# Hybrid trunk layer: first modulation blocks loaded ahead of the first weights, and S5 output products taking turns on the two row halves

## The chip, the cores and the metric

The kernel runs on one core of a Trainium2 chip. The metric is device time in microseconds (us), from the first to the last instruction of the core and the little that lies around it; the median of several runs counts, and lower is better. The engines named below are TensorE (PE, with its weight loads PEld), VectorE (DVE), ScalarE (ACT), GpSimd (POOL) and SyncE (SP, which issues nearly all transfers). Each engine works through its own instructions in a fixed order; a wait of one instruction holds everything behind it on that engine.

## What is computed

One pre-norm residual layer on `x` (1024 positions, 1024 channels, float32), with adaLN modulation. Of the reference, this matters here:

```python
mod = (cond @ ada_w[l] + ada_b[l])[:, None, :]
sh1, sc1, g1, sh2, sc2, g2 = jnp.split(mod, 6, axis=-1)
u = rmsnorm(h, norm_mix_w[l]) * (1.0 + sc1) + sh1
proj = u @ w_in[l]
...
# S5: a complex diagonal scan per group, then
y = (jnp.einsum('bsgp,ghp->bsgh', st_re, c_re.astype(f32))
     - jnp.einsum('bsgp,ghp->bsgh', st_im, c_im.astype(f32)))
y = y.reshape(bsz, s, S5_WIDTH) + d_skip.astype(f32) * uf
g = jax.nn.gelu(y)
...
h = h + g1 * (groups @ w_out[l])
v = rmsnorm(h, norm_mlp_w[l]) * (1.0 + sc2) + sh2
h = h + g2 * (jnp.square(jax.nn.relu(v @ mlp_w1[l])) @ mlp_w2[l])
```

`u` feeds one input projection; its columns go to a pooling, a gated convolution, an SSD and an S5 mixer, whose outputs are concatenated, projected and followed by an MLP.

## The kernel before

Every float32 product is made of three products of rounded halves: operands are split into a high part (`uh`, `wh_...`, a cast, mostly on ACT) and the remainder (`ul`, `wl_...`, a subtraction on DVE), and PE computes high x high, high x low and low x high. A Tile scheduler orders the instructions of each engine, from the code's order, priorities and its own estimate of times; `tc.issue_after(i)` says that what is inside is to be placed behind instruction `i`, `tc.high_priority()` that it goes ahead of what else is ready.

In order of time:

- 0 to about 100 us, the x projection. Rows 0 to 511 of `x` (tiles `x0` to `x3`, `h=0`) are normalised on DVE, then for each of eight channel blocks `k` two blocks of the modulation matrix (`ada1_k`, the scale, and `ada0_k`, the shift) are reduced on DVE (`ada_block`, L326), `modulation` makes `amul` (L337) and `ash` (L339), `modulated_T` transposes the four x tiles on PE into `tp_u` (L363), ACT makes `uh` (L365) and the unrounded `t32` (L368), DVE `ul` (L371), and PE runs the products `pjx` (L638 to L640) with the weights of `split_xw` (L590). Then the same for rows 512 to 1023 (`h=1`, tiles `x4` to `x7`). Their normalisation needs a square sum on ACT and a power on POOL (`rs_u`, L347 and L348). Within `h=1` each `k` also reduces two more modulation blocks (`ada2_k`, `ada4_k`). Beside all this DVE works off some hundred small operations (`s5_small`: `s5ar`, `elo`, `ehi`, ...) for the S5 tables.
- 100 to about 260 us, the other projections (`pjs`, `zp`, `pjpl`, `pjgc`, `pjgh`, `pjgb`) and between them the two halves `b=0` and `b=1` of the S5 channels (`s5_half`): input products into `s5sr` and `s5si`, a scan on DVE that yields `s5xr` and `s5xi`, output products into the banks `s5y{b}0` and `s5y{b}1`, a GELU (`s5sq`, `s5th`, `s5g` on ACT and DVE), transposes `s5gp`, and the GLU. A bank `s5y{b}{g2}` takes, for each of four `q`, two products with 64 contraction rows (X0: L503, X1: L504; rows 0 to 63 for `g2=0` and 64 to 127 for `g2=1`) and a 128-row product T (L505).
- 260 to about 400 us, the SSD chunks (`sdd`, `sds`, `sdt`, `sy`) among the output projection `o` (L959 to L961). Sums of squares for the group norms are narrow products `bss` (L851).
- 400 us to the end, the MLP.

Loads go through SP's queue in the order of issue: before the change `ws_x0` (the first weights), then `ada1_0`, `ada0_0`, `ws_x1` and so on.

Of the kernel before, what the change touches and what calls it, by code (L numbers as in the profile page):

```python
# [21 lines left out]
P = 128  # L22
# [29 lines left out]
def body(ctx: ExitStack, tc: tile.TileContext, x, c, pk, adaT, w_x, w_zd, w_pl, w_gl, w_in, w_out, w1, w2, fnw, out):  # L52
    nc = tc.nc
    V, A, PE, G, SY = nc.vector, nc.scalar, nc.tensor, nc.gpsimd, nc.sync
# [14 lines left out]
    def bank(name, tag="ms"):  # L69
        return pp.tile([P, 512], F32, tag=tag, name=name)  # L70
# [25 lines left out]
    xt = [gran(f"x{tb}", tag="x") for tb in range(NB)]  # L96
# [212 lines left out]
    for h in range(2):  # L309
        ps = bank(f"cb{h}", "pj")  # L310
# [8 lines left out]
    def ada_load(s, j, tag="m"):  # L319
        t = gran(f"ada{s}_{j}", tag=tag)  # L320
        lastload[0] = SY.dma_start(out=t, in_=adaT[s * 8 + j])
        return t

    def ada_block(s, j, t):
        col = mod[:, s * 8 + j:s * 8 + j + 1]
        V.scalar_tensor_tensor(out=t, in0=t, scalar=0.5, in1=cond, op0=MUL, op1=MUL, accum_out=col)  # L326

    amul = small("amul", 8)
    ash = small("ash", 8)
# [5 lines left out]
    def modulation(s_sh, s_sc, j, mulcol, shcol, wname):  # L335
        i, k = s_sc * 8 + j, s_sh * 8 + j
        V.scalar_tensor_tensor(out=mulcol[:, j:j + 1], in0=mod[:, i:i + 1], scalar=adab1[:, i:i + 1],  # L337
                               in1=pv(wname, j, j + 1), op0=ADD, op1=MUL)
        V.tensor_tensor(out=shcol[:, j:j + 1], in0=mod[:, k:k + 1], in1=pv("ada_b", k, k + 1), op=ADD)  # L339
# [19 lines left out]
    def modulated_T(n, k, h, mulcol, shcol, hi, lo, nm, act, t=None):  # L359

        ps = bank(f"tp_{nm}{k}{h}")
        for t4 in range(4):
            PE.transpose(ps[:, t4 * P:(t4 + 1) * P], n[h * 4 + t4][:, k * P:(k + 1) * P], ident)  # L363
        m, b = mulcol[:, k:k + 1], shcol[:, k:k + 1]
        A.activation(out=hi[:, H[h]], in_=ps, func=AF.Identity, scale=m, bias=b)  # L365
        t = t or half(f"t32_{nm}{k}{h}")
        if act:
            A.activation(out=t, in_=ps, func=AF.Identity, scale=m, bias=b)  # L368
        else:
            V.tensor_scalar(out=t, in0=ps, scalar1=m, scalar2=b, op0=MUL, op1=ADD)  # L370
        return V.tensor_tensor(out=lo[:, H[h]], in0=t, in1=f(hi[:, H[h]]), op=SUB)  # L371
# [91 lines left out]
    def s5_half(b, tables, Vb, GT):  # L463

        WT, CP, T, (ct, st) = tables
        ug = lambda g: Vb[:, g * P:(g + 1) * P]
        Zr, Zi, t1, t2 = (half(f"s5{n}{b}") for n in ("zr", "zi", "t1", "t2"))
        pr, pi = bank(f"s5sr{b}"), bank(f"s5si{b}")
        for q in range(4):
            for g2 in range(2):  # L470
                for w_, o in ((WT[0], pr), (WT[1], pi)):
                    PE.matmul(o[64 * g2:64 * g2 + 64, q * P:(q + 1) * P],
                              w_[:, q * P + 64 * g2:q * P + 64 * g2 + 64], ug(2 * q + g2), start=True, stop=True)
        tt(pr, ct, MUL, o=t1)
        tt(pi, st, MUL, o=t2)
        tt(t1, t2, ADD, o=Zr)
        tt(pi, ct, MUL, o=t1)
        tt(pr, st, MUL, o=t2)
        tt(t1, t2, SUB, o=Zi)
        for z in (Zr, Zi):  # L480
            for q in range(4):
                sl = slice(q * P, (q + 1) * P)
                V.tensor_tensor_scan(out=z[:, sl], data0=prm["mag8"][:, 4 * b + q:4 * b + q + 1].to_broadcast([P, P]),
                                     data1=z[:, sl], initial=0.0, op0=MUL, op1=ADD)

        q3 = lambda t: t.rearrange("p (q c) -> p q c", q=4)
        X = [half(f"s5xr{b}"), half(f"s5xi{b}")]
        for xx, a, c_, op in ((X[0], ct, st, SUB), (X[1], st, ct, ADD)):
            V.memset(q3(xx)[:, :, 0:1], 0.0)
            tt(Zr, a, MUL, o=t1)  # L490
            tt(Zi, c_, MUL, o=t2)
            last = V.tensor_tensor(out=q3(xx)[:, :, 1:128], in0=q3(t1)[:, :, 0:127], in1=q3(t2)[:, :, 0:127], op=op)
        Gs = gran(f"s5g{b}", tag="g5")
        c0 = math.sqrt(2.0 / math.pi)
        v8 = lambda t: t.rearrange("p (i e) -> p i e", i=8)

        for g2 in range(2):
            ps = bank(f"s5y{b}{g2}")
            s_ = slice(64 * g2, 64 * g2 + 64)
            for q in range(4):  # L500
                o = ps.rearrange("p (i g e) -> p i g e", i=8, g=4)[:, :, q, :]
                qs = slice(q * P, (q + 1) * P)
                PE.matmul(o, X[0][s_, qs], CP[0][s_, qs], start=True, stop=False)  # L503
                PE.matmul(o, X[1][s_, qs], CP[1][s_, qs], start=False, stop=False)  # L504
                PE.matmul(o, ug(2 * q + g2), T[g2][:, qs], start=False, stop=True)  # L505

            a_, b_ = half(f"s5sq{b}{g2}"), half(f"s5th{b}{g2}")
            A.activation(out=a_, in_=ps, func=AF.Square)
            V.tensor_scalar(out=a_, in0=a_, scalar1=0.044715 * c0, scalar2=c0, op0=MUL, op1=ADD)
            tt(a_, ps, MUL, o=b_)  # L510
            A.activation(out=b_, in_=b_, func=AF.Tanh)
            V.scalar_tensor_tensor(out=v8(Gs)[:, :, g2 * 64:(g2 + 1) * 64], in0=v8(b_), scalar=1.0, in1=v8(ps),
                                   op0=ADD, op1=MUL)
        gt3 = GT.rearrange("p (c i) -> p i c", i=8)
        for h in range(2):
            ps = bank(f"s5gp{b}{h}")
            for i4 in range(4):
                i = h * 4 + i4
                PE.transpose(ps[:, i4 * P:(i4 + 1) * P], Gs[:, i * P:(i + 1) * P], ident)
            A.copy(out=gt3[:, h * 4:(h + 1) * 4, :], in_=ps.rearrange("p (i c) -> p i c", i=4))  # L520
        return last
# [53 lines left out]
    def load_xw(k):  # L575
        t = wp.tile([P, 1024], F32, tag="ws", name=f"ws_x{k}", bufs=2)
        SY.dma_start(out=t[:, 0:768], in_=w_x[k])
        return t
# [18 lines left out]
    ada_tag = ("m", "g5")  # L597
    uh = [gran(f"uh{k}", F32R, "u") for k in range(NB)] if False else []
    ul = []
    ready(range(4))  # L600
    xb = []
    for h in range(2):
        if h == 0:
            ps = [bank(f"pjx{i}{h}", "pj" if i < 4 else "ms") for i in range(NX)]
        for k in range(NB):
            if h == 0:
                t = load_xw(k)
                ab = [ada_load(e, k, ada_tag[e]) for e in (1, 0)]
                if k == XAT:
                    with tc.issue_after(lastload[0].ins):  # L610
                        load_x(range(4, NB))
                split_xw(k, t)
                for e in (1, 0):
                    ada_block(e, k, ab[1 - e])
                modulation(0, 1, k, amul, ash, "nw")
                uh.append(gran(f"uh{k}", F32R, "u"))
                ul.append(gran(f"ul{k}", F32R, "u"))
            elif k == 0:
                with tc.issue_after(lastload[0].ins):
                    if XAT >= NB:  # L620
                        load_x(range(4, NB))
                    SY.dma_start(out=pk2, in_=pk[:, first:])
                    plw = small("plw", 256)
                    SY.dma_start(out=plw, in_=w_pl)
                ready(range(4, NB))
            modulated_T(xt, k, h, amul, ash, uh[k], ul[k], "u", True)
            if h == 1 and k == 0:
                for i in range(NX):
                    xb.append(gran(f"xb{i}", tag="x" if i < 4 else "m"))
                    A.copy(out=xb[i][:, H[0]], in_=ps[i])  # L630
                ps = [bank(f"pjx{i}{h}", "pj" if i < 4 else "ms") for i in range(NX)]
            if h == 1:
                for e in (2, 4):
                    ada_block(e, k, ada_load(e, k, "g5"))
            for i in range(NX):
                wh, wl, o = xw_of(k, i)
                c_ = slice(o, o + P)
                PE.matmul(ps[i], wh[:, c_], uh[k][:, H[h]], start=(k == 0), stop=False)  # L638
                PE.matmul(ps[i], wh[:, c_], ul[k][:, H[h]], start=False, stop=False)
                PE.matmul(ps[i], wl[:, c_], uh[k][:, H[h]], start=False, stop=(k == NB - 1))  # L640
# [27 lines left out]
    for b in range(2):  # L668
        ps = proj(8 + b, f"s5{b}")
# [13 lines left out]
    for q in range(8):  # L683
        ps = bank(f"zp{q}", "pj")
        o, ts_ = ps[:, 0:NZ], slice(q * P, (q + 1) * P)
# [78 lines left out]
    ps = bank("sfx")  # L764
# [15 lines left out]
    for q in range(8):  # L780
# [5 lines left out]
        for src, nm in ((ah, "Rh"), (al, "Rl")):  # L786
            o = half(f"{nm}{q}", F32R)
# [717 lines left out]
```

## Time and profile before

| what | value |
| --- | --- |
| runs | 1039.15, 1042.04, 1044.17 us; median 1042.04 us |
| profiled execution | 1042.58 us, of which 1040.7 us are the span from first to last instruction (1.9 us lie around it) |
| mean granted TensorE clock | 0.997 |
| PE busy | 1007.8 us (97% of the span) |
| DVE busy | 767.8 us (74%) |
| ACT, POOL busy | 497.9 us (48%), 48.4 us (5%) |

The span is nearly all PE. So the rows to look for are those where PE idles, and behind each of them the instruction that it waited for. In a timeline a row gives start, busy time, engine, line, operation, tiles without buffer numbers, shapes, the count of records put together, and in brackets the idle time before it and what ended that.

### The profile page before, as it was taken

How to read it: one execution, taken by the hardware profiler on the slowest of the kernel's cores; microseconds unless marked ns; L12 is line 12 of the kernel's file. 1: busy time of each engine (PE TensorE's matmuls, PEld its weight loads, DVE VectorE, ACT ScalarE, POOL GpSimd, SP SyncE). 2: the span in 40 equal slices, each digit the busy share in tenths (PEclk: the TensorE clock that was granted, in tenths of full speed). 3: DMA queues.
4: the chain of work that ended last, by engine and by line, in shares of the span. 5: the costliest groups of instructions: out<-in, count | busy, mean ns of one | idle time of the engine just before them, and what ended most of it. 6: DMA issues, size and time to landing. Idle time of an engine off the chain costs nothing.

```text
span 1040.7 us, 13216 instructions
## 1 busy us (share of the span) xinstructions
PE 1007.8 (97%) x4790; PEld 824.7 (79%) x4790; DVE 767.8 (74%) x1361; ACT 497.9 (48%) x825; POOL 48.4 (5%) x80
## 2 busy tenths in 40 slices
PE   4999999999999999999999999999999999999997
PEld 2777897776888888788888888887888888787886
DVE  8999959777788778986667667556644866567884
ACT  5644622315743426765556556564443443433642
POOL 2200000000020112000000000000000000000031
PEclk9999999999999999999999999999999999999999
DMA  9973311125321124145545554378975466787112
GB/s 362 335 259 126 101 45 41 61 64 172 130 114 41 41 75 168 31 152 182 182 163 194 189 186 147 134 300 307 386 280 186 144 200 209 254 305 257 43 52 110
DMA packets 62179, 175.07 MB, mean 168 GB/s; under 512 B 6529, under 2 KB 11137, under 8 KB 62114
## 3 DMA queue, kind: packets, MB, share of 16 engines
q1 hardware_dynamic: 61474, 173.07, 48.1%
q10 hardware_dynamic: 576, 1.05, 0.3%
q8 instruction: 37, 0.61, 0.2%
q14 instruction: 28, 0.23, 0.1%
q0 software_dynamic: 64, 0.11, 0.0%
HBM read 135.17 MB, written 39.04 MB: 167 GB/s over the span
## 4 chain that ended last, share of the span: by engine, by line
PE 77%; DVE 10%; DMA 8%; issue 2%; ACT 2%; POOL 0%; SPq 0%; POOLq 0%; DVEq 0%; ACTq 0%
PE q L1085 6%; PE q L1086 6%; PE q L1084 6%; PE px L1084 5%; PE px L1086 5%; PE px L1085 5%; DMA b12T<-in_w_dram 3%; DMA b21B<-in_w_dram 3%; PE o L959 3%; PE o L960 3%; PE o L961 3%; PE pz L1084 2%; PE pz L1086 2%; PE pz L1085 2%; DVE ada L326 2%; PE pjgh L547 2%
## 5 line engine op out<-in xcount | busy, mean ns | idle before, releaser
L1085 PE MATMUL q<-l_BT,h_AS 128*128 128x512 f32 x192 | 75.2, 392 | 1.2 <-DVE l_BT L1011 1.2
L1086 PE MATMUL q<-h_BT,l_AS 128*128 128x512 f32 x192 | 74.7, 389 | 0.0
L1010 ACT CAST h_AS<-aS 128x1024 fp32r<-128x1024 f32 x32 | 33.6, 1054 | 84.3 <-PE q L1085 69.9
L1084 PE MATMUL q<-h_BT,h_AS 128*128 128x512 f32 x192 | 64.0, 389 | 0.0
L1011 DVE TENSOR_TENSOR woS<-w,woS 128x512 fp32r<-128x512 f32 x60 | 41.2, 691 | 30.7 <-ACT woS L1010 30.7
L1010 ACT CAST woS<-w 128x512 fp32r<-128x512 f32 x60 | 37.2, 624 | 49.7 <-PE px L1086 25.6
L1011 DVE TENSOR_TENSOR l_A<-a,h_A 128x1024 fp32r<-128x1024 f32 x24 | 29.4, 1224 | 38.2 <-ACT h_A L1010 35.1
L1011 DVE TENSOR_TENSOR l_AS<-aS,h_AS 128x1024 fp32r<-128x1024 f32 x32 | 39.0, 1222 | 19.2 <-ACT h_AS L1010 18.9
L959 PE MATMUL o<-wh_wo,yh 128*128 128x512 f32 x128 | 52.5, 410 | 0.1
L960 PE MATMUL o<-wl_wo,yh 128*128 128x512 f32 x128 | 51.8, 405 | 0.0
L961 PE MATMUL o<-wh_wo,yl 128*128 128x512 f32 x128 | 50.8, 401 | 0.0
L1010 ACT CAST h_A<-a 128x1024 fp32r<-128x1024 f32 x24 | 25.2, 1052 | 53.0 <-PE q L1085 44.2
L1085 PE MATMUL q<-l_BB,h_A 128*128 128x512 f32 x128 | 50.0, 391 | 0.5 <-DVE l_BB L1011 0.5
L1086 PE MATMUL q<-h_BB,l_A 128*128 128x512 f32 x128 | 49.8, 389 | 0.0
L138 DVE TENSOR_TENSOR u<-u,pz 128x512 f32<-128x512 f32 x30 | 20.6, 687 | 39.1 <-ACT u L1156 29.0
L1084 PE MATMUL px<-vT,woS 128*128 128x512 f32 x120 | 46.8, 390 | 0.0
L1086 PE MATMUL px<-vT,woS 128*128 128x512 f32 x120 | 46.7, 389 | 0.0
L1085 PE MATMUL px<-vT,woS 128*128 128x512 f32 x120 | 46.7, 389 | 0.0
L966 DVE SCALAR_TENSOR_TENSOR h<-o,br,h 128x512 f32<-128x512 f32 x48 | 35.8, 748 | 11.5 <-PE o L961 11.2
L1085 PEld LDWEIGHTS q<-l_BT,h_AS 128*128 128x128 f32 x192 | 36.0, 188 | 10.2 <-DVE l_BT L1011 2.8
L1084 PE MATMUL q<-h_BB,h_A 128*128 128x512 f32 x128 | 42.6, 390 | 0.6 <-ACT h_BB L1010 0.6
L1010 ACT CAST wo<-w 128x512 fp32r<-128x512 f32 x45 | 27.8, 624 | 30.6 <-PE pz L1086 16.6
(513 smaller groups left out, 2934.0 us busy)
## 6 DMA issues: line engine op xcount, KB each, us to landing
ada<-in_ada_dram SPq DMA_DIRECT2D x32, 512.0 KB, 5.1
aS<-spS SPq DMA_DIRECT2D x32, 512.0 KB, 4.3
w<-in_w_dram SPq DMA_DIRECT2D x30, 512.0 KB, 3.5
spS<-s SPq DMA_DIRECT2D x48, 256.0 KB, 2.2
a<-sp SPq DMA_DIRECT2D x24, 512.0 KB, 5.7
b21B<-in_w_dram SPq DMA_DIRECT2D x16, 512.0 KB, 6.8
b22T<-in_w_dram SPq DMA_DIRECT2D x16, 512.0 KB, 3.6
sp<-u SPq DMA_DIRECT2D x30, 256.0 KB, 2.0
```

The lines of the kernel that those rows point to most:

```text
L138: (eng or V).tensor_tensor(out=o, in0=a, in1=b, op=op)
L326: V.scalar_tensor_tensor(out=t, in0=t, scalar=0.5, in1=cond, op0=MUL, op1=MUL, accum_out=col)
L547: PE.matmul(ps[h], w_[:, ks], u_[:, H[h]], start=(a and first), stop=(b and last))
L959: PE.matmul(ps, yh_, wo[b][0][:, H[h]], start=(b == 0), stop=False)
L960: PE.matmul(ps, yh_, wo[b][1][:, H[h]], start=False, stop=False)
L961: PE.matmul(ps, yl_, wo[b][0][:, H[h]], start=False, stop=(b == 1))
L966: V.scalar_tensor_tensor(out=hh, in0=ps, scalar=r[:, tb:tb + 1], in1=hh, op0=MUL, op1=ADD)
L1010: A.copy(out=hi, in_=t)
L1011: return V.tensor_tensor(out=lo, in0=t, in1=f(hi), op=SUB)
L1084: PE.matmul(ps, wh, ub, start=first, stop=False, skip_group_check=more)
L1085: PE.matmul(ps, wh, lb, start=False, stop=False, skip_group_check=more)
L1086: PE.matmul(ps, wl, ub, start=False, stop=last, skip_group_check=more)
```

## The change

Three edits. First, for `k=0` the two modulation blocks are loaded ahead of the first weights, and `modulation` of `h=0` runs at high priority. Second, for `h=1` the reductions of `ada2_k` and `ada4_k` are placed behind `ul_k` of the same block (the loads are issued as before). Third, both S5 output banks are allocated first; for `b=0` the X products of the two row halves take turns for each `q`, followed by both T products; for `b=1` the order stays (bank by bank), but all products are written ahead of the GELU code.

```diff
+        banks_ = [bank(f"s5y{b}{g2}") for g2 in range(2)]
+        outs = [[ps.rearrange("p (i g e) -> p i g e", i=8, g=4)[:, :, q, :] for q in range(4)] for ps in banks_]
+        if b == 0:
+            steps = [[(q, 0), (q, 1)] for q in range(4)]
+        else:
+            steps = [[(q, g2)] for g2 in range(2) for q in range(4)]
+        for step in steps:
+            for r in range(2):
+                for q, g2 in step:
+                    s_, qs = slice(64 * g2, 64 * g2 + 64), slice(q * P, (q + 1) * P)
+                    PE.matmul(outs[g2][q], X[r][s_, qs], CP[r][s_, qs], start=(r == 0), stop=False)
+            for q, g2 in step:
+                PE.matmul(outs[g2][q], ug(2 * q + g2), T[g2][:, q * P:(q + 1) * P], start=False, stop=True)
         for g2 in range(2):
-            ps = bank(f"s5y{b}{g2}")
-            s_ = slice(64 * g2, 64 * g2 + 64)
-            for q in range(4):
-                o = ps.rearrange("p (i g e) -> p i g e", i=8, g=4)[:, :, q, :]
-                qs = slice(q * P, (q + 1) * P)
-                PE.matmul(o, X[0][s_, qs], CP[0][s_, qs], start=True, stop=False)
-                PE.matmul(o, X[1][s_, qs], CP[1][s_, qs], start=False, stop=False)
-                PE.matmul(o, ug(2 * q + g2), T[g2][:, qs], start=False, stop=True)
+            ps = banks_[g2]
...
+                if k == 0:
+                    ab = [ada_load(e, k, ada_tag[e]) for e in (1, 0)]
                 t = load_xw(k)
-                ab = [ada_load(e, k, ada_tag[e]) for e in (1, 0)]
+                if k:
+                    ab = [ada_load(e, k, ada_tag[e]) for e in (1, 0)]
...
-                modulation(0, 1, k, amul, ash, "nw")
+                with tc.high_priority():
+                    modulation(0, 1, k, amul, ash, "nw")
...
-            modulated_T(xt, k, h, amul, ash, uh[k], ul[k], "u", True)
+            lo_ = modulated_T(xt, k, h, amul, ash, uh[k], ul[k], "u", True)
...
             if h == 1:
-                for e in (2, 4):
-                    ada_block(e, k, ada_load(e, k, "g5"))
+                ab = [ada_load(e, k, "g5") for e in (2, 4)]
+                with tc.issue_after(lo_.ins):
+                    for e in (2, 4):
+                        ada_block(e, k, ab[e // 2 - 1])
```

The scheduler reorders more than these lines; no engine's number of instructions or columns changes. Lines of the changed kernel are 7 higher from L513 on and 14 higher behind the x projection's loop (L503 to L505 become L508 and L510).

DVE at the start, before: the first weights' low parts, `x3`, the two blocks, then the second weights' low parts ahead of `ash`.

```order
L590 TENSOR_TENSOR wl_x0_380<-ws_x0_372,wh_x0_378 128x512
L138 TENSOR_TENSOR s5ar0_91<-s5ar0_91 128x8
L571 TENSOR_SCALAR x3_82<-x3_82,rs_u3_362 128x1024
L153 SCALAR_TENSOR_TENSOR s5ar0_91<-s5ar0_91 128x8
L590 TENSOR_TENSOR wl_y0_381<-ws_x0_372,wh_y0_379 128x256
L326 SCALAR_TENSOR_TENSOR ada1_0_374,mod_323<-ada1_0_374,cond_314 128x1024
...
L326 SCALAR_TENSOR_TENSOR ada0_0_376,mod_323<-ada0_0_376,cond_314 128x1024
L337 SCALAR_TENSOR_TENSOR amul_324<-mod_323,adab1_328,pkt_72 128x1
L153 SCALAR_TENSOR_TENSOR s5ar0_91<-s5ar0_91 128x8 x3
L590 TENSOR_TENSOR wl_x0_380<-ws_x1_419,wh_x0_378 128x512
L590 TENSOR_TENSOR wl_y0_381<-ws_x1_419,wh_y0_379 128x256
L339 TENSOR_TENSOR ash_325<-mod_323,pkt_72 128x1
```

And now: one low part of the first weights stands ahead of `ash`, the other and both of the second weights behind it.

```order
L326 SCALAR_TENSOR_TENSOR ada1_0_372,mod_323<-ada1_0_372,cond_314 128x1024
L145 TENSOR_SCALAR s5ar0_91<-s5ar0_91 128x8 x2
L578 TENSOR_SCALAR x3_82<-x3_82,rs_u3_362 128x1024
L337 SCALAR_TENSOR_TENSOR amul_324<-mod_323,adab1_328,pkt_72 128x1
L153 SCALAR_TENSOR_TENSOR s5ar0_91<-s5ar0_91 128x8
L326 SCALAR_TENSOR_TENSOR ada0_0_374,mod_323<-ada0_0_374,cond_314 128x1024
L138 TENSOR_TENSOR s5ar0_91<-s5ar0_91 128x8
L153 SCALAR_TENSOR_TENSOR s5ar0_91<-s5ar0_91 128x8
L597 TENSOR_TENSOR wl_x0_380<-ws_x0_376,wh_x0_378 128x512
L339 TENSOR_TENSOR ash_325<-mod_323,pkt_72 128x1
L597 TENSOR_TENSOR wl_y0_381<-ws_x0_376,wh_y0_379 128x256
```

PE at the S5 output products of `b=0`, now, from the first X1 on (before, all of bank `s5y00` stood ahead of the rest of `s5y01`, each `q` as X0, X1, T):

```order
L508 MATMUL s5y00_1620<-cpi0_1483,s5xi0_1610 128x8x16
L508 MATMUL s5y01_1621<-cpi0_1483,s5xi0_1610 128x8x16
L510 MATMUL s5y00_1620<-toep00_1511,s5v0_1075 128x8x16
L510 MATMUL s5y01_1621<-toep10_1513,s5v0_1075 128x8x16
L508 MATMUL s5y00_1620<-cpr0_1482,s5xr0_1609 128x8x16
L508 MATMUL s5y01_1621<-cpr0_1482,s5xr0_1609 128x8x16
L508 MATMUL s5y00_1620<-cpi0_1483,s5xi0_1610 128x8x16
L508 MATMUL s5y01_1621<-cpi0_1483,s5xi0_1610 128x8x16
```

Neighbours now lie in different row halves, and two T products follow each other.

DVE at the end of the GELU of `b=1`, before: the second half of `s5g1`, for which the transposes `s5gp10` on PE wait, stands behind a multiplication that needs the finished projection `pjgh10`.

```order
L138 TENSOR_TENSOR s5th11_1832<-s5sq11_1831,s5y11_1818 128x512
L326 SCALAR_TENSOR_TENSOR ws_ada3_6_2784,mod_323<-ws_ada3_6_2784,cond_314 128x1024
L138 TENSOR_TENSOR gq1_2701<-gq1_2701,pjgh10_2711 128x512
L512 SCALAR_TENSOR_TENSOR s5g1_1797<-s5th11_1832,s5y11_1818 128x8x64
L138 TENSOR_TENSOR gq1_2701<-gq1_2701,pjgh11_2712 128x512
```

And now the two have changed places.

```order
L138 TENSOR_TENSOR s5th11_1832<-s5sq11_1831,s5y11_1799 128x512
L326 SCALAR_TENSOR_TENSOR ws_ada3_6_2784,mod_323<-ws_ada3_6_2784,cond_314 128x1024
L519 SCALAR_TENSOR_TENSOR s5g1_1797<-s5th11_1832,s5y11_1799 128x8x64
L138 TENSOR_TENSOR gq1_2701<-gq1_2701,pjgh10_2711 128x512
L138 TENSOR_TENSOR gq1_2701<-gq1_2701,pjgh11_2712 128x512
```

Three more moves count. On PE the transpose of `x7` for `k=0` of `h=1` now stands behind eight products of `uh6` and `ul6`, where it stood directly behind that of `x6`. On DVE, eight of the blocks `ada2_k` and `ada4_k` stood ahead of `ul1` of `h=1`; now two do, but 40 small operations of the S5 tables more. And in front of the output projection the narrow products `bss`, `sy` and `sds`, which formed one run, now have wide products among them (three of `sdd2`, five of `pjgb`).

## Rows read from the trace of the kernel before

**Rows 1.** Busy time by stretch (us; PE, PEld, DVE, ACT, POOL), clock, DMA share, GB/s.

```profile
20.00:40.00 20.00, 20.00 (x92) 16.52 (x92) 20.00 (x71) 9.94 (x18) 0.00 (x0) 1.00 0.99 370
```

**Rows 2.** Waits of PE: operation, what it waited for, us in total, times, longest.

```profile
PE pjx L639 <- DVE ul L371: 1.7, 1, 1.7
...
PE s5gp L519 <- DVE s5g L512: 1.2, 1, 1.2
...
PE pjgh L547 <- ACT wh_gh L113: 0.6, 1, 0.6
```

**Rows 3.** Timeline of DVE from 12.4 to 18.4 us.

```profile
14.27 1.22 DVE L326 SCALAR_TENSOR_TENSOR ada<-ada,cond 128x1024 f32<-128x1024 f32 x1
...
15.63 1.22 DVE L326 SCALAR_TENSOR_TENSOR ada<-ada,cond 128x1024 f32<-128x1024 f32 x1
...
17.14 0.69 DVE L590 TENSOR_TENSOR wl_x<-ws_x,wh_x 128x512 fp32r<-128x512 f32 x1
17.74 0.42 DVE L590 TENSOR_TENSOR wl_y<-ws_x,wh_y 128x256 fp32r<-128x256 f32 x1
18.08 0.15 DVE L339 TENSOR_TENSOR ash<-mod,pkt 128x1 f32<-128x1 f32 x1
```

**Rows 4.** Timeline of PE from 13 to 23.7 us.

```profile
19.16 2.07 PE L638 MATMUL pjx<-uh,wh_x 128*128 128x512 f32 x4 [4.69 <-ACT uh L365]
```

**Rows 5.** Timeline of all engines around the transpose of x7.

```profile
49.52 0.55 POOL L348 TENSOR_TENSOR rs_u<-rs_u,mhalf 128x1 f32<-128x1 f32 x1
50.11 0.75 DVE L571 TENSOR_SCALAR x<-x,rs_u 128x1024 f32<-128x1024 f32 x1 [0.50 <-POOL rs_u L348]
...
50.92 0.33 PE L363 MATMUL tp_u<-pkt,x 128*128 128x128 f32 x1 [1.36 <-DVE x L571]
```

**Rows 6.** Timeline of all engines around ul1 of the second rows.

```profile
67.30 1.23 DVE L326 SCALAR_TENSOR_TENSOR ada<-ada,cond 128x1024 f32<-128x1024 f32 x1 [1.03 <-DMA ada<-in_ada_dram]
...
68.45 0.69 DVE L371 TENSOR_TENSOR ul<-t_u,uh 128x512 fp32r<-128x512 f32 x1
...
69.19 0.50 PE L639 MATMUL pjx<-ul,wh_x 128*128 128x512 f32 x1 [1.69 <-DVE ul L371]
```

**Rows 7.** Timeline of DVE at small operations, two in a row.

```profile
100.52 0.17 DVE L138 TENSOR_TENSOR ehis<-s5ar 128x8 f32<-128x8 f32 x1
100.61 0.17 DVE L138 TENSOR_TENSOR s5ar<-s5ar 128x8 f32<-128x8 f32 x1
100.81 0.17 DVE L147 TENSOR_SCALAR s5ar<-s5ar 128x8 f32<-128x8 f32 x1
```

**Rows 8.** Timeline of PE at the S5 output products, first half of the channels.

```profile
173.78 0.49 PE L503 MATMUL s5y<-cpr,s5xr 64*128 64x128 f32 x4
...
175.85 0.48 PE L504 MATMUL s5y<-cpi,s5xi 64*128 64x128 f32 x2
176.26 0.49 PE L505 MATMUL s5y<-toep,s5v 128*128 128x128 f32 x2
176.68 0.48 PE L503 MATMUL s5y<-cpr,s5xr 64*128 64x128 f32 x2
...
177.74 0.48 PE L503 MATMUL s5y<-cpr,s5xr 64*128 64x128 f32 x2
...
183.68 0.71 PE L547 MATMUL pjgc<-uh,wl_gc 128*128 128x512 f32 x2
```

**Rows 9.** Timeline of all engines in front of the transposes s5gp10.

```profile
244.93 0.69 DVE L138 TENSOR_TENSOR gq<-gq,pjgh 128x512 f32<-128x512 f32 x1 [0.89 <-PE pjgh L547]
245.54 0.68 DVE L512 SCALAR_TENSOR_TENSOR s5g<-s5th,s5y 128x512 f32<-128x512 f32 x1
...
246.37 0.30 PE L519 MATMUL s5gp<-pkt,s5g 128*128 128x128 f32 x1 [1.24 <-DVE s5g L512]
```

**Rows 10.** Busy time by stretch, behind the narrow products (columns as in Rows 1).

```profile
289.70:293.10 3.40, 3.40 (x10) 2.65 (x9) 3.40 (x9) 0.12 (x1) 3.21 (x2) 0.50 0.70 282
```

**Rows 11.** Timeline of PE, two wide products ahead of that stretch.

```profile
289.15 0.39 PE L960 MATMUL o<-wl_wo,yh 128*128 128x512 f32 x1
289.38 0.39 PE L961 MATMUL o<-wh_wo,yl 128*128 128x512 f32 x1
```

## Prediction

> **What bounds the kernel now.** I read the table on the run first, then the busy time by stretch, the list of PE's waits, and timelines around each wait. PE is busy for 1007.8 of 1040.7 us, so a change pays only by taking out one of its waits, by making PE's own work shorter, or by keeping its clock up; DVE matters where it decides when PE goes on. It does so early: between 20 and 40 us DVE is as full as PE, 20.00 of 20.00 us [rows 1]. The list of waits then names those that the change can reach: 1.7 us on `ul`, 1.2 on `s5g`, 0.6 on `wh_gh` [rows 2], to which the timelines add the first product at 19.16, which comes after 4.69 us of idling [rows 4], and the transpose of `x7`, 1.36 us [rows 5]. From 400 us on nothing is moved, and I take that part as it is.
>
> **Edit 1, the start.** The first product waits for `uh0`, this for `ash` at 18.08 [rows 3, 4]. Ahead of `ash` go away the second weights' low parts, from 17.14 to 18.08, thus 0.94, and one `wl_y`, 0.34 by the step from 17.74 to 18.08 [rows 3], and a few small operations. `x3` and one `wl_x` stay ahead of it. That makes 1.3 to 1.6 us earlier, if the two blocks land in time: their transfers move one place forward, the first weights' two places back, and DVE stood in neither case before 14.27 waiting for them. But this lead hardly lives. DVE has no idle time from there to 40 us [rows 1], and its work ahead of the `x` tiles of the second rows isn't less. What PE gains ahead of DVE, it loses again at the next `ul` or low weights. What counts is when PE can pass the transpose of `x7`. This one waits for a DVE operation at 50.11, and that for POOL's power, from 49.52 [rows 5]. Both hang on transfers and on ACT's square sums, which the change doesn't bring forward. Alone I give the lead 0, with 1.6 as the other end.
>
> **The transpose of x7.** Now eight products stand in front of it, at 0.23 us each, the step from 289.15 to 289.38 [rows 11], thus 1.8 us. They cover the 1.36 us [rows 5] wholly if PE comes to them on time. DVE has the low parts of `k=5` later than before, because four more blocks stand ahead of `ul4` and `ul5`, at 1.15 us each (67.30 to 68.45 [rows 6]); and ACT does the square sums of three tiles behind `uh6` now. So I take 1.2, between 0.4 and 1.8 (the upper end by the eight products).
>
> **Edit 2, ul1 of the second rows.** Before, PE waits 1.69 us at 69.19 for `ul1`, behind a block for whose load DVE had waited 1.03 us [rows 6]. Ahead of `ul1` six blocks go away, 6 x 1.15 = 6.9 us, and that load wait of 1.03; 40 small operations are added. Their price is the open one: they cost 0.09 us where independent ones follow each other and 0.20 where one needs the last (100.52 to 100.61, and 100.61 to 100.81 [rows 7]), thus 3.6 to 8.0 us. `ul1` is then between 4.3 us earlier and 0.1 later. PE is itself 1.2 earlier, so it needs 2.9 to wait no longer. The new run is a ladder of squarings in pairs, some operations depending on the last and some not, nearer to the middle: 5.8 us, `ul1` 2.1 earlier. The gain is 1.69 less the 0.8 that is missing: I take 0.9, ends 0 and 1.7. The blocks that are put off come between the later `ul`; these had more time, and PE's 1.69 us stay the size of what can come back there.
>
> **Edit 3, the output products of b=0.** From 175.85 to 183.68 PE does 7.8 us of them. One `q` of one half takes 1.06 (176.68 to 177.74), of which T is 0.42 (176.26 to 176.68), so both X 0.64 [rows 8]. The row at 173.78 shows what taking turns does: there the X0 of both halves stand together by chance, and four records take 0.49 us, where elsewhere two take 0.48 [rows 8]. Products in different row halves run side by side. So X0 and X1 of both halves cost 0.64 together instead of 1.28, and the second T comes without a change from half rows to whole ones. A change is what the steps leave over: I put that T at 0.22, about half of 0.42, by which a `q` takes 1.28 instead of 2.12. Three whole `q` save 2.5, and the first, whose X0 pair exists already, 0.83 x 2 - 1.05 = 0.6. The sum is 3.1. If the second T costs 0.42 too, it is 2.3; if pairs of X behind a pair didn't overlap, about 0.8.
> [...]
>
> What this hands on: DVE must have `s5wi1` and the low weights of `pjgh` ready earlier. The GELU frees it (both banks now end together, so that it doesn't wait twice on ACT), and PE's 0.6 us on `wh_gh` [rows 2] may go, as ACT's cast now stands ahead of two copies. I expect a wait of about 1 on DVE there and the 0.6 won, together a loss of 0.4, ends 0 and 1.6 (half of what the alternation gives). The input products `s5sr` and `s5si` now change places instead of coming in runs of eight; each still has a neighbour in the other column half, so I put that at 0.
>
> **The GELU of b=1.** `s5g` started at 245.54 because DVE stood in front of `gq` until 244.93 for PE's projection [rows 9]. Now it stands ahead of that, and all that it needs has been done by then, so PE's 1.24 us [rows 9] go. I take 1.2, ends 0.6 and 1.3.
>
> **The clock.** At 289.70 the granted clock falls to 0.50, the lower of its two levels, for 3.4 us [rows 10], behind a run of narrow products; ten wide products ran there that need half as long at full clock, so 1.7 us are lost. Before, nothing wide stood in that run; now there are eight wide products among it. I take it that the clock stays up: 1.7, ends 0 and 1.7. I have one fall to go by, so this is the least sure term.
>
> **Sum.** 1.2 + 0.9 + 3.1 + 1.2 + 1.7 - 0.4 = 7.7, less 0.5 for waits on newly placed transposes (`tp_u61` comes right before its use, as `tp_u51` did): 7.2 us. From the profiled execution's 1042.58 that gives **1035.4 us**; this execution lies 0.54 above the median of the three runs, so against 1042.04 it is 6.6 us faster. What a measurement of this kernel can tell from no change is about 0.5%, 5.2 us.
>
> **Rivals.**
> 1. *DVE takes it back.* The small operations cost 0.20, so that `ul1` is no earlier; and behind the quicker output products PE waits for DVE's tables. For it speaks that DVE is full for long stretches [rows 1], against it that its waits on loads and on ACT go too. 7.2 - 0.9 - 1.2 = 5.1, and 0.8 less for a dear second T: 4.3, thus 1038.3. Chance 0.22.
> 2. *The clock falls all the same*, there or in a neighbouring stretch: 1035.4 + 1.7 = 1037.1. Against it stand only the eight wide products. Chance 0.17.
> 3. *The halves don't take turns.* Pairs behind a pair queue up, and the third edit gives 0.8: 1035.4 + 2.3 = 1037.7. The row at 173.78 [rows 8] speaks against it. Chance 0.06.
> 4. *Slower than before.* The denser narrow products of `b=0` bring the clock down in the S5 stage, as the run of `bss` did at 289.70. Each us at half clock loses 0.5 [rows 10]; so it outweighs 7.2 from 14.4 us on, four times the one stretch of the trace. With 20 us it is 1045.4. Before, the same products in the old order, nearly as narrow, left the clock at full. Chance 0.04.
> The forecast has 0.51: 1033 to 1037, from its smaller terms' ends.
>
> **Numbers.** Upwards, rivals 1 to 3 stay below 1040.5 with 1.6 us for the spread of a run; downwards, the lead of the start (1.6), the full x7 and `ul1` (1.4 together) and no waits behind (0.9) give 1031.5. So the range is 1031.5 to 1040.5. Faster by over 0.5% means below 1036.8: most of the forecast, somewhat under half of rivals 2 and 3 and a quarter of rival 1, 0.60. Slower: 0.04. The rest, 0.36, within 0.5%.
>
> **What the profile after would show.** The first product at about 17.6; no idle time ahead of the `x7` transpose; `ul1` of the second rows below 1 us of waiting; the `b=0` products 4.9 us long, with four X records at a time; no wait on `s5g` at `b=1`; PEclk at 1.00 throughout 280 to 300. I would be wrong if PE's waits on `ul`, `wl_...` or `wtpi` between 20 and 200 us add up to more than 3 us, or if the clock's falls move instead of going away.

## The result and the profile after

The changed kernel takes 1035.54 us in the median of six runs (1032.84 to 1037.33), the kernel before 1042.87 (1039.15 to 1047.42, six runs beside them): a ratio of 0.992, 95% interval [0.9902, 0.9937], so it is 0.6 to 1.0% faster. Forecast were 1035.4 us, 1031.5 to 1040.5. Its profiled execution, 1032.99 us, is among its fastest, and the only one of the six whose mean granted clock is 0.998; the others have 0.995 or 0.996, which counts below.

```profile
span 1031.2 us, 13223 instructions
PE 1003.2 (97%) x4790; PEld 822.3 (80%) x4790; DVE 767.7 (74%) x1361; ACT 497.4 (48%) x825; POOL 45.7 (4%) x80
```

PE is busy for 4.6 us less than the 1007.8 before, and the span is 9.5 us shorter; so half of the gain is shorter work and half is waiting that went. The list of PE's waits (what it waited for: us in total, times, longest) is the next view; it answers to [rows 2].

```profile
PE glu L540 <- DMA glw<-in_w_gl_dram: 0.7, 1, 0.7
...
PE pjgc L554 <- ACT wh_gc L113: 0.4, 1, 0.4
PE pjx L653 <- DVE ul L371: 0.4, 1, 0.4
```

The waits on `s5g`, `wh_gh` and `ul1` are gone; the 0.4 us on `ul` belongs to an earlier one. One wait is new: 0.7 us on the load of `glw`. The timelines (start, busy time, engine, line, operation, in brackets the idle time ahead and its releaser) go through the steps of the prediction. First the start, against [rows 3, 4]: `ash` on DVE, then the first product on PE.

```profile
17.07 0.15 DVE L339 TENSOR_TENSOR ash<-mod,pkt 128x1 f32<-128x1 f32 x1
18.15 1.22 PE L652 MATMUL pjx<-uh,wh_x 128*128 128x512 f32 x2 [2.58 <-ACT uh L365]
```

Then the passage of `x7`, against [rows 5]: no idle time ahead of its transpose (52.59, no bracket), but PE now waits 0.40 us for an `ul` and 0.32 for `x6` on the way to it.

```profile
46.74 0.50 PE L653 MATMUL pjx<-ul,wh_x 128*128 128x512 f32 x1 [0.40 <-DVE ul L371]
...
50.31 0.33 PE L363 MATMUL tp_u<-pkt,x 128*128 128x128 f32 x1 [0.32 <-DVE x L578]
...
52.59 0.27 PE L363 MATMUL tp_u<-pkt,x 128*128 128x128 f32 x1
```

`ul1` of the second rows, against [rows 6], on DVE, with the first of the small operations ahead of it:

```profile
58.58 0.16 DVE L138 TENSOR_TENSOR s5ar<-eloc 128x8 f32<-128x8 f32 x1
...
65.30 0.69 DVE L371 TENSOR_TENSOR ul<-t_u,uh 128x512 fp32r<-128x512 f32 x1
```

It starts at 65.30 instead of 68.45, and PE doesn't wait for it. From the first row on 61 operations lie ahead of `ul1`, in 6.7 us: 0.11 each. The output products of `b=0`, against [rows 8]:

```profile
173.26 0.49 PE L508 MATMUL s5y<-cpi,s5xi 64*128 64x128 f32 x4
173.68 0.71 PE L510 MATMUL s5y<-toep,s5v 128*128 128x128 f32 x4
174.32 0.49 PE L508 MATMUL s5y<-cpr,s5xr 64*128 64x128 f32 x4
174.65 0.39 PE L508 MATMUL s5y<-cpi,s5xi 64*128 64x128 f32 x4
174.97 0.71 PE L510 MATMUL s5y<-toep,s5v 128*128 128x128 f32 x4
175.61 0.49 PE L508 MATMUL s5y<-cpr,s5xr 64*128 64x128 f32 x4
...
178.01 0.70 PE L554 MATMUL pjgc<-uh,wl_gc 128*128 128x512 f32 x2
```

From 173.26 to 178.01 they take 4.75 us instead of 7.83. X comes in fours; a `q` takes 1.29 (174.32 to 175.61), of which the two X pairs 0.65 and the two T 0.64. The end of the GELU of `b=1`, against [rows 9]:

```profile
237.07 0.68 DVE L519 SCALAR_TENSOR_TENSOR s5g<-s5th,s5y 128x512 f32<-128x512 f32 x1
238.22 1.04 PE L526 MATMUL s5gp<-pkt,s5g 128*128 128x128 f32 x8
239.94 0.67 PE L540 MATMUL glu<-s5v,glw 128*128 128x512 f32 x1 [0.68 <-DMA glw<-in_w_gl_dram]
```

`s5g` starts 1.15 us ahead of its transposes, which don't wait; the first `glu` does. Last the busy time by stretch where the clock fell (us; PE, PEld, DVE, ACT, POOL; then clock, DMA share, GB/s), against [rows 10]: it stays at 1.00.

```profile
279.30:282.46 3.16, 3.16 (x27) 2.86 (x27) 3.16 (x8) 2.94 (x7) 0.49 (x1) 1.00 1.03 417
282.46:285.90 3.44, 3.44 (x22) 2.96 (x21) 3.44 (x7) 2.30 (x8) 3.36 (x4) 1.00 0.59 206
```

### The profile page after: what moved, and what is told of

The parts are those of the page before. It is cut to its first block, busy times and chain, and to the rows that moved or that the text cites. A ratio compares the mean times of both kernels' runs of the same rounds, so it can differ in the third digit from the quotient of the medians.

```text
span 1031.2 us, 13223 instructions
## 1 busy us (share of the span) xinstructions
PE 1003.2 (97%) x4790; PEld 822.3 (80%) x4790; DVE 767.7 (74%) x1361; ACT 497.4 (48%) x825; POOL 45.7 (4%) x80
## 4 chain that ended last, share of the span: by engine, by line
PE 80%; DVE 9%; DMA 7%; ACT 1%; issue 1%; SPq 0%; POOL 0%; POOLq 0%; DVEq 0%; ACTq 0%
PE q L1099 7%; PE q L1100 6%; PE q L1098 6%; PE px L1098 5%; PE px L1100 5%; PE px L1099 5%; DMA b12T<-in_w_dram 3%; PE o L973 3%; PE o L974 3%; PE o L975 3%; DMA b21B<-in_w_dram 3%; PE pz L1100 2%; PE pz L1098 2%; PE pz L1099 2%; PE pjgb L554 2%; PE pjgc L554 2%
## 5 line engine op out<-in xcount | busy, mean ns | idle before, releaser
L1098 PEld LDWEIGHTS q<-h_BT,h_AS 128*128 128x128 f32 x192 | 36.0, 188 | 7.5
```

What stands on the lines that cost most here:

```text
L1098: PE.matmul(ps, wh, ub, start=first, stop=False, skip_group_check=more)
```

## The experiments

All runs but e7 are timed in rounds with the kernel before, whose median was 1043.05 us in the first set, 1042.15 in the second and 1043.65 in the third. One execution of each was traced. The table has the start of the same work of PE in each trace, read from the timelines; the last column is the span less the start of `q`, where the program is the same in all. The traced executions of e1 and e2 are the slowest of theirs, those of e3, e4, e10 and after_again the fastest.

| traced kernel | edits | `tp_u40` | `tp_u11` | `pjs50` | first `q` | to the end |
| --- | --- | --- | --- | --- | --- | --- |
| before | none | 32.23 | 63.37 | 99.36 | 702.88 | 337.8 |
| e12_bss_before | none, bss0 later | 33.25 | 64.04 | 99.88 | 703.15 | 335.4 |
| e1_start | 1 | 30.68 | 62.31 | 102.04 | 705.52 | 337.1 |
| e2_ada | 2 | 32.99 | 64.31 | 97.56 | 702.74 | 338.4 |
| e3_turns | 3 | 33.06 | 63.71 | 98.97 | 695.12 | 336.6 |
| e4_noturns | all, no turns | 31.12 | 62.45 | 96.21 | 699.58 | 335.8 |
| changed kernel | all | 32.01 | 63.18 | 96.63 | 693.89 | 337.3 |
| after_again | all | 31.02 | 62.11 | 95.55 | 692.62 | 335.8 |
| after_third | all | 32.02 | 63.67 | 97.66 | 694.55 | 337.2 |
| e5_both | all, b=1 too | 31.34 | 62.94 | 96.68 | 698.48 | 336.6 |
| e7_glw | all, glw early | 31.12 | 62.53 | 95.83 | 695.35 | 336.7 |
| e8_snake | e7, snake | 31.40 | 62.94 | 96.37 | 694.56 | 336.1 |
| e11_bss | all, bss0 later | 31.33 | 62.92 | 96.20 | 692.92 | 337.0 |
| e10_all | e8, bss0 later | 30.57 | 62.16 | 95.41 | 690.57 | 335.4 |

The last column varies by 3.0 us although nothing there differs, and the start (`tp_u11` of the changed kernel) by 1.6 within one program. So a single trace's span can't be set against a sum of terms; stretches can.

### One edit at a time

```diff
# e1_start: the kernel before with
+                if k == 0:
+                    ab = [ada_load(e, k, ada_tag[e]) for e in (1, 0)]
                 t = load_xw(k)
...
+                with tc.high_priority():
+                    modulation(0, 1, k, amul, ash, "nw")
# e2_ada: the kernel before with
+                ab = [ada_load(e, k, "g5") for e in (2, 4)]
+                with tc.issue_after(lo_.ins):
+                    for e in (2, 4):
+                        ada_block(e, k, ab[e // 2 - 1])
# e3_turns: the kernel before with the third edit's block
```

> Edit 1 alone (blocks of k=0 loaded first, modulation at high priority). In its order the transpose of x7 stands behind eight products, as in the changed kernel, and seven blocks stand ahead of ul1 of the second rows (eight before). Theory A, the prediction's term: the 1.36 us in front of x7 are hidden, so PE comes to tp_u11 at about 62.2 instead of 63.37, and the wait on ul1 stays between 1 and 1.7 us. Theory B: DVE is full there and sets PE's pace, so what is not waited for at x7 is waited for at an ul or an x tile shortly ahead of it: tp_u11 at 63.0 to 63.3, with one or two new waits of 0.3 to 0.5 us. The time is 0 to 1.5 us below the kernel before in both, less than the measurement tells.

Measured 1041.35 us, ratio 0.9994 [0.998, 1.0008]. PE comes to `tp_u11` at 62.31, as A has it; but the lead was there before `x7` already (30.68 at `tp_u40`), and the passage of `x7` took 0.5 of it back, as B has it. Later it lost more than it had won: blocks and the low weights of the next projections stand ahead of `ul7`, PE idles for 2.83 us, and behind that the clock is down in this trace. A timeline row of PE and two stretches of e1:

```profile
93.12 0.50 PE L644 MATMUL pjx<-ul,wh_x 128*128 128x512 f32 x1 [2.83 <-DVE ul L371]
```

```profile
89.00:93.10 4.10, 1.29 (x6) 0.72 (x4) 4.10 (x26) 1.58 (x3) 0.00 (x0) 1.00 0.18 46
93.10:97.60 4.50, 4.48 (x13) 3.53 (x14) 4.39 (x22) 0.00 (x0) 0.00 (x0) 0.62 0.21 78
```

So edit 1 by itself gives nothing that can be measured; with edit 2 the wait of 2.83 is not there.

> Edit 2 alone (ada2_k and ada4_k behind ul_k). Two blocks instead of eight stand ahead of ul1 of the second rows, 30 small operations more. Theory A, the prediction's term: the small operations cost about 0.14 us each, half of the 1.69 us wait on ul1 stays, gain 0.9 us at the first product of pjs50 (before: 99.36). Theory B: they cost nearer to 0.09, the wait goes wholly and with it the delay of the later uh and ul, so pjs50 starts 1.7 to 2.3 us earlier. The x7 wait of 1.36 stays in both. Time 0.9 (A) or about 2 us (B) below the kernel before.

Measured 1040.39 us, ratio 0.9984 [0.9972, 0.9997], which is 1.7 us; the medians differ by 2.7. From `tp_u11` to `pjs50` PE takes 33.25 us instead of 35.99 before (35.26 in e3, 35.84 in e12, which have the same order there): the whole wait on `ul1` and more, as B has it. The transposes `wtpr`, 0.4 us, have moved behind `pjs`; so 1.8 us are won. Against the kernel before the trace loses them again, since its clock is at 0.50 for 6.8 us from 285.9 on instead of 3.4.

> Edit 3 alone (products of b=0 take turns, all of b=1 written ahead of its GELU). Theory A: the b=0 products take 4.8 instead of 7.8 us (3.1), the 1.24 us wait on s5g at b=1 goes, the clock stays up where it fell (1.7), some 0.5 lost to a new wait on the load of glw: 5.5 us below the kernel before, about 1037.4. Theory B, the gain at b=1 and the clock come from the order that all three edits give together: 3.1 us alone, about 1039.8. If the clock falls all the same: 3.8 us, 1039.1, with a stretch at 0.50 near 285 us.

Measured 1035.39 us, ratio 0.994 [0.9923, 0.9957], which is 6.3 us (the medians differ by 7.7): as A has it and a little more. From `pjs50` to the first `q` it takes 596.15 us, the kernel before 603.52. Edit 3 alone has most of the change.

### The changed kernel without turns

```diff
-        if b == 0:
+        if b < 0:
             steps = [[(q, 0), (q, 1)] for q in range(4)]
```

> The changed kernel with b=0 in the order of b=1, bank by bank; all else as changed. In its order the multiplication gq at b=1 stands ahead of the second half of s5g again. Theory A, taking turns is what pays: the b=0 products take 7.8 us again (+3.1), the wait of 1.2 us on s5g returns and covers the 0.7 us on glw (+0.6), so about 3.7 us over the changed kernel, 1039.2; with the clock falling at the narrow products in front of the output projection, 1.7 more, 1040.9. Theory B, writing both banks ahead of the GELU pays by itself: less than 2 us over the changed kernel.

Measured 1038.97 us, ratio 0.9966 [0.995, 0.9982], 3.4 us over the changed kernel by the medians of two sets; 603.37 us from `pjs50` to `q`, 6.1 over the changed kernel's 597.26. Two of its waits, and a stretch where the clock is down:

```profile
PE s5gp L526 <- DVE s5g L519: 1.2, 1, 1.2
PE pjgh L554 <- ACT wh_gh L113: 0.6, 1, 0.6
```

```profile
285.80:289.30 3.50, 3.50 (x10) 2.73 (x11) 3.50 (x8) 0.09 (x1) 2.48 (x1) 0.52 0.88 353
```

All three gains beside the turns themselves (the GELU, the cast, the clock) leave with them. They aren't effects of writing both banks first, which e4 keeps: they come with the turns, behind which the scheduler orders DVE, ACT and the narrow products otherwise. B falls.

### Turns in both halves, and the clock

```diff
-        if b == 0:
+        if b < 2:
             steps = [[(q, 0), (q, 1)] for q in range(4)]
```

> The changed kernel with the products of b=1 taking turns too. Their 7.8 us become 4.7 or 4.8. Theory A: PE then waits for the GELU of b=1, since both banks end together and in its order one block more (ws_ada, and its load) stands ahead of the second half of s5g: about 2.5 of the 3.1 us come back as a wait in front of s5gp10. In front of the output projection its order has one run of 45 narrow records again (18 and 22 in the changed kernel), so the clock falls there for 3 to 5 us although the products take turns: 1.5 to 2.5 us more. Sum: 1 to 2 us over the changed kernel. Theory B: taking turns is what keeps the clock up and the GELU is hidden: 3.1 us under the changed kernel.

Measured 1036.67 us, ratio 0.994 [0.9921, 0.9959]: no gain but a loss, as A has it, only larger, 5.7 us over the changed kernel in the same set (1030.97, below). The products of `b=1` do become shorter, but PE then stands in front of their transposes (DVE's last operations ahead of them, and PE):

```profile
238.21 1.22 DVE L326 SCALAR_TENSOR_TENSOR ws_ada<-ws_ada,cond 128x1024 f32<-128x1024 f32 x1
...
239.35 0.68 DVE L519 SCALAR_TENSOR_TENSOR s5g<-s5th,s5y 128x512 f32<-128x512 f32 x1
```

```profile
240.18 1.94 PE L526 MATMUL s5gp<-pkt,s5g 128*128 128x128 f32 x8 [4.81 <-DVE ash L339]
```

The 4.81 us are put down to `ash` but end with `s5g`, behind a block that isn't needed. A had the wait, but not what came with it: the clock is at 0.50 from 237.50 on, 2.1 us into it, to 244.30, so that PE works at half clock for 4.1 us behind the wait and loses 2.1. The wait and the stretch behind it:

```profile
237.50:240.20 2.70, 0.02 (x1) 0.05 (x1) 2.70 (x7) 1.81 (x2) 0.00 (x0) 0.50 0.43 159
240.20:244.30 4.10, 4.10 (x11) 2.73 (x12) 3.48 (x4) 3.34 (x5) 0.00 (x0) 0.50 0.60 170
```

And with 45 narrow records together the clock falls though the products take turns (0.51 in its stretch from 285.4 to 288.8).

### The load of glw

```diff
-        glw = half("glw")
+        glw = half("glw", tag="t")
```

> The changed kernel with the load of glw in a buffer of another pool, which moves it on SP's queue from behind six loads of ws_ada to ahead of them; nothing else in the order of any engine changes. Theory A: the 0.68 us in front of the first glu are late issue, so the wait goes, and glu starts 0.9 us behind the first s5gp10 instead of 1.7; the loads of ws_ada behind it come 1.5 us or so later, which DVE's wait of 0.35 on one of them may show. Theory B: the transfer itself is late because the DMA engines are busy: a wait stays.

Measured 1034.13 us in one run. The load is issued at 205 instead of 234.8, and PE goes from the transposes straight to `glu`:

```profile
237.42 1.04 PE L526 MATMUL s5gp<-pkt,s5g 128*128 128x128 f32 x8
238.30 3.17 PE L540 MATMUL glu<-s5v,glw 128*128 128x512 f32 x7
```

So A holds: late issue, 0.8 us. But then, with PE's order the same, the clock falls where it stayed up in the changed kernel. Three stretches of e7:

```profile
278.38:282.29 3.91, 3.91 (x24) 3.91 (x22) 3.91 (x8) 3.69 (x12) 2.03 (x2) 0.59 1.02 398
282.29:285.85 3.56, 3.56 (x11) 2.68 (x11) 2.78 (x5) 0.75 (x3) 2.51 (x3) 0.50 0.27 78
285.85:289.30 3.45, 3.45 (x20) 2.98 (x19) 3.23 (x8) 0.37 (x1) 0.00 (x0) 0.99 0.35 134
```

It costs 3.2 us: against the changed kernel e7 is 1.71 us early ahead of this place and 1.47 late behind it.

### Fewer changes between half and whole rows

```diff
# and the load of glw as in e7
+        for n, step in enumerate(steps):
+            t1st = n % 2 == 1
+            if t1st:
+                for q, g2 in step:
+                    tm(q, g2, True)      # T
             for r in range(2):
                 for q, g2 in step:
+                    xp(q, g2, r, t1st)   # X
+            if not t1st:
+                for q, g2 in step:
+                    tm(q, g2, False)
```

> The load of glw as in e7, and in both halves every second step does T ahead of X instead of behind it, so that X follows X and T follows T: of the changes between half rows and whole ones 3 of 7 go at b=0 and 8 of 15 at b=1. Theory A, each change costs what separates a first record from a repeated one, 0.2 us: b=0 takes 4.1 instead of 4.75 us, b=1 6.1 instead of 7.8, and the glw wait of 0.7 is gone; PE may wait up to 1 us for s5g at b=1. 2 to 3 us under the changed kernel. Theory B, the changes cost nothing and the 0.22 of the second T was overlap of its own: no gain at b=0 and b=1, 0.7 us under it.

Measured 1032.18 us, ratio 0.9899 [0.9879, 0.9919]. The products of `b=0` in e8:

```profile
173.00 0.49 PE L504 MATMUL s5y<-cpi,s5xi 64*128 64x128 f32 x4
173.42 1.16 PE L507 MATMUL s5y<-toep,s5v 128*128 128x128 f32 x8
174.51 0.49 PE L504 MATMUL s5y<-cpr,s5xr 64*128 64x128 f32 x4
174.83 0.39 PE L504 MATMUL s5y<-cpi,s5xi 64*128 64x128 f32 x4
175.06 0.39 PE L504 MATMUL s5y<-cpr,s5xr 64*128 64x128 f32 x4
175.28 0.39 PE L504 MATMUL s5y<-cpi,s5xi 64*128 64x128 f32 x4
...
177.33 0.73 PE L562 MATMUL pjgc<-uh,wl_gc 128*128 128x512 f32 x2
```

They take 4.33 us instead of 4.75, those of `b=1` 6.43 instead of 7.83 (224.87 to 231.30, and 225.52 to 233.35). So A holds, and its 0.2 us for a change too: four T and four pairs of X, two `q`, take 2.18 (173.42 to 175.60), where two `q` of the changed kernel take 2 x 1.29 with two changes more. Both halves gain less than A had because the expectation overlooked that the products now end with X, a change more in front of the wide product behind them: 2 changes fewer at `b=0`, 6 at `b=1`, where in addition two X1 run side by side (0.2). The gain of 2.3 us up to the first `pjgb10` (it starts 165.1 us behind `pjs50`, 167.3 in the changed kernel) doesn't show against the changed kernel, because e8's trace has e7's fall of the clock, 0.50 from 279.1 to 285.9.

### The changed kernel again, and the narrow products apart

> The changed kernel once more, for a second trace of it beside the others on the same chip. What belongs to the order of the instructions returns: b=0 in 4.75 us, no wait on ul1, no wait on s5g at b=1, 0.5 to 0.9 us on the load of glw, clock 1.00 from 280 to 300. What belongs to one execution's loads does not: the first product between 17.2 and 18.2, and by the start of tp_u11 a lead of 0.2 to 1.2 us over the kernel before.

Measured 1030.97 us (1030.18 to 1033.38), ratio 0.9891 [0.9871, 0.991].

> The changed kernel a third time, beside e11 and e10 on their chip. If it is near the edge, its six runs lie in two groups some 3 us apart or all in one of them, and its trace shows the clock at 1.00 or a stretch of about 6.5 us at 0.50 from 279 on, as e7 did with the same order of TensorE.

Measured 1033.44 us (four runs, 1031.02 to 1035.10), ratio 0.9894 [0.9877, 0.9911]. Both traces show the clock at 1.00 from 272 to 300, no wait on `ul1` or `s5g`, 0.35 and 0.51 on `glw`, and starts 1.6 us apart. The four runs' mean clocks are 0.994, 0.997, 0.999 and 0.999, and the run of 1035.10 is that of 0.994.

The traces show how to read such a mean. The six with no fall between 30 and 1000 us (e3, e10, e11 and the three of the changed kernel) have 0.998 or 0.999, the three with one of 3.4 us there 0.997 (before, e4, e12), the five with more at 0.50 have 0.994 to 0.996 (e1, e2, e5, e7, e8). By this reading seven of the sixteen runs of the changed kernel have no fall and nine have one or more: five of six in the first set, two of six in the second, two of four in the third. Within a set the runs with a fall are 2.0 to 2.5 us longer in the mean.

```diff
-    pa, ra = prepare(0, ya), norm_of(0, ya, EPS, "m")
-    project(pd, rd)
+    pa = prepare(0, ya)
+    ra = []
+    project(pd, rd, lambda tb: ra.append(norm_of(0, ya, EPS, "m")) if tb == 3 else None)
```

> The changed kernel with the square sums bss0 put four row blocks later into the output projection, so that wide products o stand where the 22 narrow records stood together (now 6, and 18 behind the o products); nothing earlier moves. Theory A, whether the clock falls in front of the output projection hangs on the narrow records standing together, and the changed kernel is near the edge, so that its executions differ by a fall: clock 1.00 from 270 to 300, runs closer together than the 4.5 us of the changed kernel's first six, and the median 1 to 2 us lower, at that of its best runs. Theory B, the spread comes from elsewhere (loads, the last stage): the same median and spread as the changed kernel.

Measured 1031.35 us (1030.51 to 1032.12), ratio 0.9875 [0.9861, 0.9889], with 0.998 or 0.999 in all four runs. PE in front of the output projection, in the changed kernel and then in e11:

```profile
278.27 1.18 PE L865 MATMUL bss<-one,sq 128*128 128x1 f32 x10
279.31 0.48 PE L807 MATMUL sdd<-Rh,mgr 128*128 128x512 f32 x1
...
280.09 2.06 PE L865 MATMUL bss<-one,sq 128*128 128x1 f32 x18
282.01 0.69 PE L813 MATMUL sds<-xa,xb 128*128 128x128 f32 x4
```

```profile
278.36 0.48 PE L807 MATMUL sdd<-Rh,mgr 128*128 128x512 f32 x1
...
279.14 0.28 PE L865 MATMUL bss<-one,sq 128*128 128x1 f32 x2
279.28 0.48 PE L973 MATMUL o<-wh_wo,yh 128*128 128x512 f32 x1
```

2.1 us under the changed kernel beside it and a spread of 1.6 instead of 4.1 us, as A has it. With four runs each the two intervals still overlap; what tells for A is the clock, with no fall by the mean in any of the four.

> e8 with bss0 moved as in e11. Theory A: the fall that e8 showed (6.5 us at 0.50, 3.2 us) goes, so 2.5 to 3.2 us under e8's 1032.2 and 2 to 2.5 under e11, the gain of the snake order and the load of glw. Theory B, the fall in e8 comes from being earlier, whatever stands there: it stays, and the time is e8's.

Measured 1030.61 us (1027.83 to 1031.50), ratio 0.9864 [0.9847, 0.988], clock 0.998 or 0.999. The fall of e8 is gone (1.00 from 262 to 320), so B falls. `pjs50` to `q` takes 595.16 us, against 596.72 in e11 and 598.19 in e8. A's sizes aren't reached: 1.6 us under e8 by the medians of two sets, and 0.7 under e11, which four runs don't tell apart (1.6 in the stretch; PE waits 0.38 for `s5g`). Against the changed kernel it is 2.8 us.

> The kernel before with bss0 moved as in e11 and none of the change. Of its run of 45 narrow records 29 stay together and 16 stand behind twelve wide products. Theory A: the clock stays up where it fell to 0.50 for 3.4 us, 1.7 us under the kernel before, 1040.5 to 1041. Theory B: 29 together are enough for a fall: same time as before, with a stretch at 0.50 near 287.

Measured 1041.12 us, ratio 0.9973 [0.9962, 0.9984], 2.5 us by the medians, and yet its trace has the fall, 0.50 for 3.4 us from 288.2 on: 29 records together are enough, as B has it, and `pjs50` to `q` is only 0.25 us shorter. Its other runs aren't all like that: the mean clock of the twelve is 0.9966, that of the 17 of the kernel before 0.9953, and three of the twelve have 0.998 or 0.999, none of the 17. An estimate from the two means is 0.0013 x 1043 = 1.4 us of shorter falls, so by this A holds in some executions. The rest of the median's gain stays open.

## Why the prediction was right, and where its terms were not

The total was right, the change does what it says, and most of it is the third edit. But the total's closeness (1035.54 for 1035.4) is partly luck: without a fall of the clock the terms give more than forecast, and most of the first six runs had one.

- **Start lead, 0, and x7, 1.2.** Their sum holds, their parts don't. With edit 1 (ten traces) `tp_u40` starts at 31.26 in the mean, without it (four) at 32.88; at `tp_u11` it is 62.72 and 63.86. So the lead lives, 1.6 us, where I said that PE loses it at the next `ul` or low weights, and at `x7` PE gives back 0.5 rather than win 1.2: what was one wait of 1.36 is now waits for `ul` and `x6` just ahead, and the same 20 transposes stand in one group more, with a longer step at its ends (0.31 instead of 0.23). Together 1.1. The first product is at 17.70 in the mean of ten (forecast 17.6).
- **ul1, 0.9, and new waits, -0.5.** Too small. The small operations cost 0.11, nearer to 0.09 than to the middle that I took, so `ul1` is 3.15 us earlier and not 2.1, and the whole wait goes; no wait for a transpose came. From `tp_u11` to `pjs50` the ten traces with edit 2 take 33.5, the three with neither edit 35.7; less the 0.4 of moved transposes 1.8 us, forecast 0.4.
- **The products of b=0, 3.1.** 3.1. The second T costs 0.22, as put down there. But the two causes share it otherwise than I had it. The turns leave 7 changes between half and whole rows of 15, at e8's 0.2 us a change 1.6, and seven pairs of X run beside another, 0.22 each, 1.5; of the 2.3 that I took for running side by side (the 3.1 with a second T at 0.42), 0.8 were changes saved. The 0.22 for that T was my estimate; the steps that show a change's price are e8's.
- **Handed on, -0.4.** -0.1, by other parts. PE's 0.6 on `wh_gh` went as expected, but the wait of 1 on `s5wi1` or the low weights never came. A wait came later, on a load that I hadn't looked at: `glw`, 0.7, because it stands on SP's queue behind six loads that wait for DVE (222.34 to 234.72 in the changed kernel; e7); 0.6 - 0.7 is left.
- **The GELU of b=1, 1.2.** 1.2, and by the cause named: e4 puts `gq` ahead of `s5g` again, and the 1.2 are back.
- **The clock, 1.7.** 1.7 in the profiled execution. In slices of 0.1 us the trace of the kernel before has 1.00 or 0.50 in all but two, in which it changes, and the step of the wide products is 0.43 at 0.50 (289.94 to 290.37), where it is 0.23 at 1.00. For the cause, narrow products without wide ones among them, speak e5 (turns, 45 together, 0.51) and e10 against e8 (1.00 against 0.50). But it isn't safe: rival 2 is what e7 and e8 show with the same order of these products, and by the mean clocks nine of the sixteen runs of the changed kernel. So the forecast and that rival are both true of it, in different executions.

Rivals 1, 3 and 4 fall: DVE took nothing back between 100 and 200 us, X overlaps in every `q` (four records in 0.33, 174.32 to 174.65, where two took 0.33), and no trace shows a fall of the clock at the products of `b=0`; the one in the S5 stage, in e5, comes in a wait of 4.81 us. Of the signs of being wrong, PE's waits on `ul` between 20 and 200 us add up to 0.4 us (1.6 in after_third), under the 3. In sum: 2.7 us up to `pjs50` (3.1 less the moved transposes; forecast 1.6) and from there to `q` 6.4 (603.4 in the three traces with neither turns nor edit 2, 597.1 in three of the changed kernel), of which 0.4 are the moved transposes, so 6.8 where the forecast had 5.6. The terms as measured, 3.1 + 0.6 - 0.7 + 1.2 + 1.7, give 5.9 of them; the other 0.9 isn't taken apart here. Together that is 9.5 us without a fall of the clock, where 7.2 was forecast, and 6.3 with one like e7's. The medians' 7.3, and 11.2 and 10.2 beside the kernel before in the later sets, lie about these two, with the spread of the start and of the end on top, and with falls that differ in the kernel before too (mean clocks from 0.992 to 0.998). No trace of the changed kernel itself shows a fall; for its untraced runs their mean clocks are all there is.

## What to carry to other kernels

Products with 64 rows of contraction paid twice here: they ran side by side in the two row halves (1.5 of the 3.1 us), and each change between half and whole rows cost 0.2 us by e8 (1.6 of the 3.1), so put like to like as well. A gain on TensorE is worth what the next late thing leaves of it: look beyond the engines for loads that stand on a queue behind waiting ones (`glw`, 0.7 us), and don't shorten work whose result another engine finishes (`b=1` in e5, a wait of 4.81 us). And keep narrow products apart by wide ones with a margin, since one order (18 and 22 narrow records, three wide ones between) kept the clock at 1.00 in four traces and not in two.

## What the hardware showed that I had not expected

- The clock falls while TensorE has no idle time, behind narrow products: behind 45 together in about 5 us it is at 0.50 for 3.4 us (before, e1, e4, e5) or 6.8 (e2, where the fall begins within them). With 18 and 22 and three wide ones between, it stayed at 1.00 in four traces and fell in two (e7, e8), for 6.8 us, with the same order; with 18 and 2 it stayed up in both traces.
- What decides between two executions of one order no run here shows.
- In e1 the clock is at 1.00 all through 2.83 us of idling and at 0.50 for 3.4 us behind the first products after it; in e5 it is at 0.50 from 2.1 us into 4.81 us of idling to 4.1 us behind their end.
